# Gates and branch outputs of a hybrid decoder layer: the tokens' chunks as the stationary operand, 512 columns of weights moving

## The chip, the core and the metric

The kernel runs on one core of a Trainium2 chip. TensorE multiplies (a stationary operand of 128 by 128 is loaded, a moving operand streams past it, the result lands in PSUM); VectorE (DVE) and ScalarE (ACT) do elementwise work; SyncE (SP) issues the DMA transfers. The metric is the device time of one execution in microseconds (us).

## The reference, cut to what matters

One layer over 256 tokens with a model width of 2048, all in float32:

```python
mod = silu(c) @ w_ada + b_ada                       # six vectors of 2048
h = rmsnorm(x) * (1 + sc1) + sh1
proj = h @ w_in                                     # mixers' operands, then 3 * 2048 gate logits
y_pool, y_sb, y_gla = three mixers                  # widths 512, 1024, 512
gates = sigmoid(gate_logits)                        # (256, 3, 2048)
merged = gates[0] * (y_pool @ w_br_pool) + gates[1] * (y_sb @ w_br_sb) + gates[2] * (y_gla @ w_br_gla)
x = x + ga1 * (merged @ w_out)
h = rmsnorm(x) * (1 + sc2) + sh2
x = x + ga2 * ((silu(h @ w_ff_gate) * (h @ w_ff_up)) @ w_ff_down)
```

## The kernel before, in words

Activations are kept transposed: channels on the 128 partitions, 256 tokens along the free dimension. Each float32 operand is split into two float32r parts, hi and lo, and a product is the sum of three matmuls (hi·hi, hi·lo, lo·hi).

A piece of weights is at most 128 x 1056 (mostly 128 x 1024, 512 KB). `load` (L65) takes one of 6 raw buffers and issues the transfer on SP; `split_w` (L71) copies it to one of 3 hi buffers on ACT (L77) and subtracts into one of 3 lo buffers on DVE (L78). A raw buffer comes free when both are done, a hi or lo buffer when TensorE has used it up.

The stages, in the order of the program:
- the first norm with its modulation, and the mixers' operands (L205 to L277);
- `proj_v(w_vg, 528)` (L533), which already has the tokens' chunks as stationary operand, with 264 columns moving;
- the branch gates (`gates`, L558): 16 groups j of three blocks; a block of 128 gate columns is `block` (L94): 16 chunks of channels, three matmuls each with the weights stationary and 256 tokens moving, in one PSUM bank `acc` (4 banks). The first 8 groups (LEAD = 8) run ahead of the branch outputs, and the steps of the three mixers run between their blocks (`steps`);
- the loop over j (L592): the gates of group j + 8 (for j below 8), two pieces of w_br, 48 matmuls of 256 columns into three regions, three multiplications by the gates and two additions of 256 columns on DVE (L603 to L607), `split_x`, and the next of the modulation's columns;
- the output projection (L611 on, `block2`, whose matmuls are 512 and 256 columns wide in turn), the second norm, the feed-forward.

The modulation's remaining 128 pieces (`ada`, L181) are threaded through these stages. Each is a load of 512 KB into a raw buffer and one multiply-and-reduce on DVE (L173). `ADA = (1, 1, 4, 1, 1)` gives their numbers: one for each gate block, four after each branch output while j is below 8, one after that.

The order of instructions on each engine comes from a scheduler at compile time, which takes them by their place in the program as their inputs are ready by its own model; loads are issued on SP in program order as raw buffers come free. Each engine then runs its queue in that order.

Of the kernel before, what the change touches and what calls it, by code (L numbers as in the profile page):

```python
# [14 lines left out]
P = 128  # L15
# [11 lines left out]
# columns of the packed per-partition vectors  # L27
# [4 lines left out]
def kernel(ctx: ExitStack, tc: tile.TileContext, xT, c, vecs, consts, invc, masks, w_ada, w_per, w_ext,  # L32
# [38 lines left out]
    def split_w(src):  # L71
        """A weight piece as hi + lo, each exact in float32r."""
        n = src.shape[-1]
        raw = load(src)
        hi = whi.tile([P, WW], F32R, tag="hi", name=f"hi{next(names)}")[:, :n]
        lo = wlo.tile([P, WW], F32R, tag="lo", name=f"lo{next(names)}")[:, :n]
        nc.scalar.copy(hi, raw)  # L77
        vec.tensor_tensor(lo, raw, hi.bitcast(F32), ALU.subtract)  # L78
        return hi, lo

    def split_x(src, hi_scale=None):
        """[hi | lo] of a [128, 256] operand."""
        t = slot(F32R)
        nc.scalar.copy(t[:, :T], src)
        vec.tensor_tensor(t[:, T:], src, t[:, :T].bitcast(F32), ALU.subtract)
        return t
# [7 lines left out]
    def block(srcs, xs):  # L94
        """One 128-column block of a product: its transposed result in PSUM."""
        a = acc()
        n, i = len(xs), 0
        for src in srcs:
            hi, lo = split_w(src)
            for k in range(src.shape[-1] // P):  # L100
                mm3(a[:, :T], hi, lo, k, xs[i], i == 0, i == n - 1)
                i += 1
        assert i == n
        return a[:, :T]

    def mm2(out, hi, lo, k, x, first, last):
        """As mm3, in two terms that lie side by side and are still to be added."""
        mm(out, lhsT=hi[:, k * P:(k + 1) * P], rhs=x, start=first, stop=False, skip_group_check=True)  # L108
        mm(out[:, :T], lhsT=lo[:, k * P:(k + 1) * P], rhs=x[:, :T], start=False, stop=last, skip_group_check=True)  # L109
# [12 lines left out]
    def add_scaled(x, a, g):  # L122
        """x + g * a for a of two terms."""
        vec.scalar_tensor_tensor(x, a[:, T:], g, x, ALU.mult, ALU.add)
        vec.scalar_tensor_tensor(x, a[:, :T], g, x, ALU.mult, ALU.add)

    def rsqrt(m, t=None):
        """(m + eps) ** -0.5 of a mean of squares in PSUM, after one Newton step."""
        n = m.shape[-1]
        r, t = slot()[:, :n], (slot() if t is None else t)[:, :n]  # L130
        act(r, m, AF.Ln, bias=eps)
        act(r, r, AF.Exp, scale=-0.5)
        act(t, r, AF.Square)
        vec.scalar_tensor_tensor(t, m, EPS, t, ALU.add, ALU.mult)
        vec.tensor_scalar(t, t, -0.5, 1.5, ALU.mult, ALU.add)
        vec.tensor_tensor(r, r, t, ALU.mult)
        return r

# [66 lines left out]
    # ---- modulation of the first norm, chunk by chunk, and the columns of the mixers' operands: six pairs of  # L205
    # 128-column blocks stay in PSUM over all chunks, fourteen are summed in SBUF over groups of four chunks ----
# [161 lines left out]
    def odd(t, L):  # L368
        """The odd ones of the runs of L positions, for two heads of two blocks."""
        return t.rearrange("p (n two l) -> p n two l", two=2, l=L)[:, :, 1, :]  # L370

    def select(p, lv, k, q):
        """Scores of the pairs of positions that a level covers, for two heads of two blocks."""
        m = mx()
        w = q.shape[-1] // 4
        for i in range(4):
            mm(m[:, i * w:(i + 1) * w], lhsT=k[:, i * P:(i + 1) * P], rhs=q[:, i * w:(i + 1) * w], start=True,  # L377
               stop=True)
        mask, sc = mk[:, lv, :], scores[p]
        if w == P:  # L380
            sc, m = (t.rearrange("p (i t) -> p i t", i=4) for t in (sc, m))
            vec.copy_predicated(sc, mask.unsqueeze(1).broadcast_to([P, 4, P]), m)
        else:
            L = LEVELS[lv]
            n = w // L
            for i in range(4):
                vec.copy_predicated(odd(sc[:, i * P:(i + 1) * P], L), odd(mask, L),
                                    m[:, i * w:(i + 1) * w].rearrange("p (n l) -> p n l", l=L))
        left[p] -= 1
# [94 lines left out]
    # every mixer is a chain of steps; a step goes in two blocks or more after the one that feeds it  # L484
# [6 lines left out]
    LEAD, LIVE, LAG, ST, ST2 = 8, 5, 1, 3, 2  # L491
# [25 lines left out]
    def proj(n):  # L517
        return block([w_gate[n, 0], w_gate[n, 1]], h)

    def proj_v(src, n):  # L520
        """128 tokens by n columns, twice: the tokens' chunks as the stationary operand."""
        w = n if n <= 512 else n // 2
        m = [[acc() for _ in range(n // w)] for _ in range(2)]
        for i in range(8):
            hi, lo = split_w(src[i])
            for kk in range(2):
                k = 2 * i + kk
                for b in range(2):
                    xh, xl = h[k][:, b * P:(b + 1) * P], h[k][:, T + b * P:T + (b + 1) * P]
                    for xs, ws, f, l in ((xh, hi, k == 0, False), (xh, lo, False, False), (xl, hi, False, k == NK - 1)):  # L530
                        for c in range(n // w):
                            o = kk * n + c * w
                            mm(m[b][c][:, :w], lhsT=xs, rhs=ws[:, o:o + w], start=f, stop=l)  # L533
            if i % 2:
                steps(ST)
            ada(ADA[4])
# [6 lines left out]
    # v of the linear attention, with the 16 columns of its decay's rank behind it  # L543
    m = proj_v(w_vg, 528)
# [11 lines left out]
    merged, sigs = [], {}  # L556

    def gates(j):  # L558
        if j < NK:
            sigs[j] = []  # L560
            for i in range(3):
                r = proj(3 * j + i)
                if len(halves) < 1:
                    s = slot()
                    halves.extend((s[:, :T], s[:, T:]))
                s = halves.popleft()
                if unfinished():
                    nc.scalar.copy(s, r)
                    raw.append(s)
                else:  # L570
                    sigmoid[0] = act(s, r, AF.Sigmoid)
                ada(ADA[0] if j < LEAD else ADA[1])
                sigs[j].append(s)
                if unfinished():
                    steps(ST)

    halves, raw = deque(), []
    sigmoid = [None]
    for j in range(LEAD):
        gates(j)  # L580
# [11 lines left out]
    for j in range(NK):  # L592
        gates(j + LEAD)
        sig = sigs[j]
        hl = [split_w(w_br[j, i]) for i in range(2)]
        brs = [acc(), acc()]
        outs = [brs[0][:, :T], brs[0][:, T:], brs[1][:, :T]]
        for kk in range(NK):
            hi, lo = hl[kk // 8]
            b, lo_k, hi_k = (0, 0, 4) if kk < 4 else (1, 4, 12) if kk < 12 else (2, 12, 16)  # L600
            mm3(outs[b], hi, lo, kk % 8, ys[kk], kk == lo_k and b != 1, kk == hi_k - 1)
        m, t = slot(), slot()
        vec.tensor_tensor(m[:, :T], outs[0], sig[0], ALU.mult)  # L603
        vec.tensor_tensor(t[:, :T], outs[1], sig[1], ALU.mult)
        vec.tensor_tensor(m[:, :T], m[:, :T], t[:, :T], ALU.add)
        vec.tensor_tensor(t[:, :T], outs[2], sig[2], ALU.mult)
        vec.tensor_tensor(m[:, :T], m[:, :T], t[:, :T], ALU.add)  # L607
        merged.append(split_x(m[:, :T]))
        ada(ADA[2] if j + LEAD < NK else j < NK - 2)

# [1 line left out]
    with tc.issue_after(sigmoid[0].ins):  # L612
        nc.scalar.preload_act_table_set("natural_log_exp_and_others")
    # the first two blocks leave their last chunk, which is ready last, to the end
    firsts = [acc(), acc()]
    held = []
    for j in range(2):
        for half in range(2):
            hi, lo = split_w(w_out[j, half])
            for k in range(8 - half):  # L620
                mm2(firsts[j], hi, lo, k, merged[8 * half + k], k + half == 0, False)
        held.append((hi, lo))
    for j in range(2):
        mm2(firsts[j], *held[j], 7, merged[NK - 1], False, True)
# [43 lines left out]
    # the first three blocks go chunk by chunk, as the norm's chunks come  # L668
# [22 lines left out]
def _layouts(i):  # L691
# [5 lines left out]
    def blocks(w):  # L697
        """[K, N] -> [N/128][2][128][K/2 by 128]: per block of columns, the partition's rows in one run."""
# [3 lines left out]
    def cols(v):  # L702
# [18 lines left out]
    # pairs of 128 columns: q and k of each stick-breaking head, then q, k of the linear attention by two heads,  # L721
    # v of the stick-breaking heads, r of the linear attention and the channels of the pooling, two by two
# [14 lines left out]
        blocks(w_in[:, 5648:].reshape(D, 3, NK, P).transpose(0, 2, 1, 3).reshape(D, 3 * D)),  # L737
# [3 lines left out]
        blocks(w_br),  # L741
# [26 lines left out]
```

## Time and profile before

| | us |
|---|---|
| runs of the kernel: median of 3 (lowest, highest) | 1562.27 (1559.63, 1563.06) |
| profiled execution: span from first to last instruction | 1558.6 |
| median over this span | 3.7 |
| TensorE busy in the span | 1518.9 (97%) |
| VectorE busy | 1130.8 (73%) |
| ScalarE busy | 739.7 (47%) |

The trace gives the profiled execution by its span; no device time of its own is listed beside the three runs. The median of the runs lies 3.7 us above the span. Busy times count an instruction from start to end; matmuls are pipelined, so that a matmul's own duration is longer than the distance to the next one. The pace of a stretch is read from the starts.

### The profile page before, as it was taken

The page shows a single profiled execution, that of the slowest core. Times are in us where ns is not written, and L with a number is a line of the kernel's source. Part 1 is how long each engine was busy: PE and PEld are TensorE (multiplying, and loading weights), DVE is VectorE, ACT ScalarE, POOL GpSimd, SP SyncE. Part 2 cuts the span into 40 slices and gives each one's busy share as a digit, 9 for nine tenths or more (in the row PEclk, how much of TensorE's full clock was granted, in tenths as well). Part 3 has the DMA queues.
Part 4 walks back from the last instruction along what each step waited for, and adds up shares of the span by engine and source line. Part 5 has one row for each costly group of instructions (what it writes and reads, how often), then busy time and mean ns, then how long its engine had stood idle before and what let it go on. Part 6 is the DMA issues. An engine that isn't in the chain of part 4 may idle for free.

```text
span 1558.6 us, 26019 instructions
## 1 busy us (share of the span) xinstructions
PE 1518.9 (97%) x10304; PEld 1398.8 (90%) x10304; DVE 1130.8 (73%) x1671; ACT 739.7 (47%) x1028; POOL 1.9 (0%) x11
## 2 busy tenths in 40 slices
PE   5899999989999999999989999999999999999999
PEld 4899998989999999999877888888888888888888
DVE  7889979988877889898878666665555555545443
ACT  4454456465565434444445444444444444333333
POOL 0000000000000000000000000000000000000000
PEclk9899999999999999999999999999999999999999
DMA  9999984855768999997865777776666665666663
GB/s 329 372 328 326 332 276 136 287 193 194 243 215 280 323 342 345 351 314 230 285 208 196 234 239 229 241 230 188 189 189 189 188 189 176 207 192 202 190 207 95
DMA packets 108556, 377.17 MB, mean 242 GB/s; under 512 B 12049, under 2 KB 15249, under 8 KB 108433
## 3 DMA queue, kind: packets, MB, share of 16 engines
q1 hardware_dynamic: 108434, 375.52, 73.5%
q8 instruction: 80, 1.31, 0.3%
q14 instruction: 42, 0.34, 0.1%
HBM read 373.37 MB, written 2.10 MB: 241 GB/s over the span
## 4 chain that ended last, share of the span: by engine, by line
PE 91%; DVE 4%; DMA 2%; ACT 1%; issue 1%; SPq 0%; DVEq 0%; ACTq 0%
PE acc L108 34%; PE acc L109 18%; PE acc L92 9%; PE acc L90 9%; PE acc L91 9%; PE mx L90 3%; PE mx L91 3%; PE mx L92 3%; PE mx L239 3%; DVE raw L173 1%; PE acc L533 1%; DVE lo L78 1%; PE mx L377 1%; DMA raw<-in_w_ada_dram 1%; ACT s L39 1%
## 5 line engine op out<-in xcount | busy, mean ns | idle before, releaser
L78 DVE TENSOR_TENSOR lo<-raw,hi 128x1024 fp32r<-128x1024 f32 (+2 forms) x528 | 627.4, 1190 | 316.9 <-ACT hi L77 315.5
L77 ACT CAST hi<-raw 128x1024 fp32r<-128x1024 f32 (+2 forms) x528 | 539.3, 1023 | 653.6 <-issue 208.4
L108 PE MATMUL acc<-s,hi 128*128 128x512 f32 x2308 | 806.6, 394 | 5.5 <-DVE s L652 4.4
L109 PE MATMUL acc<-s,lo 128*128 128x256 f32 x2308 | 650.1, 282 | 1.2 <-DVE lo L78 1.1
L108 PEld LDWEIGHTS acc<-s,hi 128*128 128x128 f32 x2308 | 434.1, 188 | 104.5 <-issue 4.7
L109 PEld LDWEIGHTS acc<-s,lo 128*128 128x128 f32 x2308 | 434.7, 188 | 2.3 <-DVE lo L78 2.1
L90 PE MATMUL acc<-s,hi 128*128 128x256 f32 x1212 | 346.3, 286 | 14.2 <-ACT hi L77 14.1
L92 PE MATMUL acc<-s,lo 128*128 128x256 f32 x1212 | 344.6, 285 | 0.9 <-DVE lo L78 0.9
L91 PE MATMUL acc<-s,hi 128*128 128x256 f32 x1212 | 343.5, 284 | 0.0
L90 PEld LDWEIGHTS acc<-s,hi 128*128 128x128 f32 x1212 | 232.0, 191 | 16.3 <-ACT hi L77 15.6
L92 PEld LDWEIGHTS acc<-s,lo 128*128 128x128 f32 x1212 | 231.3, 191 | 2.9 <-DVE lo L78 2.2
L91 PEld LDWEIGHTS acc<-s,hi 128*128 128x128 f32 x1212 | 231.5, 191 | 0.2 <-issue 0.2
L173 DVE CUSTOM_DVE_ANT_0 raw<-raw,cs,mod 128x1024 f32<-128x1024 f32 x96 | 122.9, 1280 | 35.9 <-DMA raw<-in_w_ada_dram 35.1
L173 DVE CUSTOM_DVE_ANT_0 raw<-raw,cs,vt 128x1024 f32<-128x1024 f32 x96 | 122.8, 1279 | 29.3 <-DMA raw<-in_w_ada_dram 29.0
L90 PE MATMUL mx<-s,hi 128*128 128x256 f32 x384 | 110.0, 287 | 0.0
L91 PE MATMUL mx<-s,hi 128*128 128x256 f32 x384 | 108.3, 282 | 0.0
L92 PE MATMUL mx<-s,lo 128*128 128x256 f32 x384 | 108.0, 282 | 0.0
L39 ACT ACTIVATE s<-s 128x256 f32<-128x256 f32 (+2 forms) x167 | 83.5, 518 | 48.3 <-DVE s L662 34.7
L90 PEld LDWEIGHTS mx<-s,hi 128*128 128x128 f32 x384 | 73.2, 191 | 0.7 <-issue 0.5
L91 PEld LDWEIGHTS mx<-s,hi 128*128 128x128 f32 x384 | 72.8, 190 | 0.7 <-issue 0.7
L92 PEld LDWEIGHTS mx<-s,lo 128*128 128x128 f32 x384 | 72.7, 190 | 0.0
L239 PE MATMUL mx<-hi,s 128*128 128x256 f32 x256 | 47.4, 282 | 0.7 <-DVE s L302 0.7
(133 smaller groups left out, 780.5 us busy)
## 6 DMA issues: line engine op xcount, KB each, us to landing
raw<-in_w_ada_dram SPq DMA_DIRECT2D x192, 512.0 KB, 4.9
raw<-in_w_ff_dram SPq DMA_DIRECT2D x176, 512.0 KB, 4.2
raw<-in_w_gate_dram SPq DMA_DIRECT2D x96, 512.0 KB, 4.7
raw<-in_w_down_dram SPq DMA_DIRECT2D x80, 512.0 KB, 4.2
raw<-in_w_ext_dram SPq DMA_DIRECT2D x56, 512.0 KB, 5.2
raw<-in_w_br_dram SPq DMA_DIRECT2D x32, 512.0 KB, 5.0
raw<-in_w_out_dram SPq DMA_DIRECT2D x32, 512.0 KB, 4.5
raw<-in_w_per_dram SPq DMA_DIRECT2D x32, 384.0 KB, 5.0
```

The source lines that it names most:

```text
L39: r = nc.scalar.activation(out, in_, func, **kw)
L77: nc.scalar.copy(hi, raw)
L78: vec.tensor_tensor(lo, raw, hi.bitcast(F32), ALU.subtract)
L90: mm(out, lhsT=wh, rhs=x[:, :T], start=first, stop=False, skip_group_check=True)
L91: mm(out, lhsT=wh, rhs=x[:, T:], start=False, stop=False, skip_group_check=True)
L92: mm(out, lhsT=wl, rhs=x[:, :T], start=False, stop=last, skip_group_check=True)
L108: mm(out, lhsT=hi[:, k * P:(k + 1) * P], rhs=x, start=first, stop=False, skip_group_check=True)
L109: mm(out[:, :T], lhsT=lo[:, k * P:(k + 1) * P], rhs=x[:, :T], start=False, stop=last, skip_group_check=True)
L173: vec.tensor_tensor_reduce(raw, raw, cs[:, i * 1024:(i + 1) * 1024], 1.0, init, ALU.mult, ALU.add, mod[:, t, i:i + 1])
L239: mm(m[:, b * T:(b + 1) * T], lhsT=l, rhs=r, start=first and i == 0, stop=last and i == 2, skip_group_check=True)
L377: mm(m[:, i * w:(i + 1) * w], lhsT=k[:, i * P:(i + 1) * P], rhs=q[:, i * w:(i + 1) * w], start=True, stop=True)
L533: mm(m[b][c][:, :w], lhsT=xs, rhs=ws[:, o:o + w], start=f, stop=l)
```

## The change

Gate logits and branch outputs are computed with the activations' chunks (128 channels by 128 tokens) as the stationary operand and 512 columns of hi or lo weights as the moving one, by a `proj_v` that takes any operand list. The results have tokens on partitions, in two banks of 512 columns. There are now 4 groups g of 512 columns in place of 16 groups of 128; two groups of gates run ahead. The mixers' steps are taken after every second piece inside `proj_v`, the modulation's pieces after every second piece of gates (`every=2`), and in the branch loop in one run after each of the three branches: 4, 8 and 4 for the first two groups, 1, 2 and 1 for the last two. The merged result is turned back, in 128 x 128 blocks, by `nc.tensor.transpose` into a PSUM bank `mx` and split from there; the turn of a group stands behind the first branch of the next one. The first two blocks of the output projection leave their last four chunks to the end, in place of the last one. The weights on the host are laid out to match, in pieces of the same size (128 x 1024).

```diff
-    def proj(n):
-        return block([w_gate[n, 0], w_gate[n, 1]], h)
-
-    def proj_v(src, n):
-        """128 tokens by n columns, twice: the tokens' chunks as the stationary operand."""
+    def proj_v(src, n, x=h, every=1):
         w = n if n <= 512 else n // 2
         m = [[acc() for _ in range(n // w)] for _ in range(2)]
-        for i in range(8):
+        last = 2 * len(src) - 1
+        for i in range(len(src)):
             hi, lo = split_w(src[i])
             for kk in range(2):
                 k = 2 * i + kk
                 for b in range(2):
-                    xh, xl = h[k][:, b * P:(b + 1) * P], h[k][:, T + b * P:T + (b + 1) * P]
-                    for xs, ws, f, l in ((xh, hi, k == 0, False), (xh, lo, False, False), (xl, hi, False, k == NK - 1)):
+                    xh, xl = x[k][:, b * P:(b + 1) * P], x[k][:, T + b * P:T + (b + 1) * P]
+                    for xs, ws, f, l in ((xh, hi, k == 0, False), (xh, lo, False, False), (xl, hi, False, k == last)):
                         for c in range(n // w):
                             o = kk * n + c * w
                             mm(m[b][c][:, :w], lhsT=xs, rhs=ws[:, o:o + w], start=f, stop=l)
-            if i % 2:
+            if i % 2 and unfinished():
                 steps(ST)
-            ada(ADA[4])
+            ada(i % every == every - 1)
         return m
...
-    def gates(j):
-        if j < NK:
-            sigs[j] = []
+    NG, LEAD_G = 4, 2
...
+    def gates(g):
+        if g < NG:
+            sigs[g] = []
             for i in range(3):
-                r = proj(3 * j + i)
-                if len(halves) < 1:
-                    s = slot()
-                    halves.extend((s[:, :T], s[:, T:]))
-                s = halves.popleft()
-                if unfinished():
-                    nc.scalar.copy(s, r)
-                    raw.append(s)
-                else:
-                    sigmoid[0] = act(s, r, AF.Sigmoid)
-                ada(ADA[0] if j < LEAD else ADA[1])
-                sigs[j].append(s)
-                if unfinished():
-                    steps(ST)
+                m = proj_v([w_gate[i, g, n] for n in range(8)], 512, every=2)
+                s = [slot(), slot()]
+                for b in range(2):
+                    if unfinished():
+                        nc.scalar.copy(s[b], m[b][0])
+                        raw.append(s[b])
+                    else:
+                        sigmoid[0] = act(s[b], m[b][0], AF.Sigmoid)
+                sigs[g].append(s)
...
-    for j in range(NK):
-        gates(j + LEAD)
-        sig = sigs[j]
-        hl = [split_w(w_br[j, i]) for i in range(2)]
-        brs = [acc(), acc()]
-        outs = [brs[0][:, :T], brs[0][:, T:], brs[1][:, :T]]
-        for kk in range(NK):
-            hi, lo = hl[kk // 8]
-            b, lo_k, hi_k = (0, 0, 4) if kk < 4 else (1, 4, 12) if kk < 12 else (2, 12, 16)
-            mm3(outs[b], hi, lo, kk % 8, ys[kk], kk == lo_k and b != 1, kk == hi_k - 1)
-        m, t = slot(), slot()
-        vec.tensor_tensor(m[:, :T], outs[0], sig[0], ALU.mult)
...
-        merged.append(split_x(m[:, :T]))
-        ada(ADA[2] if j + LEAD < NK else j < NK - 2)
+    def turn(ms, c):
+        m = mx()
+        for i in range(4):
+            nc.tensor.transpose(m[:, i * P:(i + 1) * P], ms[i % 2][:, (c + i // 2) * P:(c + i // 2 + 1) * P], ident)
+        for i in range(2):
+            merged.append(split_x(m[:, i * T:(i + 1) * T]))
+
+    waiting = []
+    for g in range(NG):
+        gates(g + LEAD_G)
+        ms = [slot(), slot()]
+        for i, (k0, k1) in enumerate(((0, 4), (4, 12), (12, 16))):
+            o = proj_v([w_br[g, n] for n in range(k0 // 2, k1 // 2)], 512, ys[k0:k1], 8)
+            ada((4 if g + LEAD_G < NG else 1) * (k1 - k0) // 4)
+            for b in range(2):
+                s = sigs[g][i][b]
+                vec.tensor_tensor(s if i else ms[b], o[b][0], s, ALU.mult)
+                if i:
+                    vec.tensor_tensor(ms[b], ms[b], s, ALU.add)
+            if i == 0:
+                while waiting:
+                    turn(*waiting.pop(0))
+        waiting += [(ms, 0), (ms, 2)]
...
-            for k in range(8 - half):
+            for k in range(8 - 4 * half):
                 mm2(firsts[j], hi, lo, k, merged[8 * half + k], k + half == 0, False)
         held.append((hi, lo))
+    while waiting:
+        turn(*waiting.pop(0))
     for j in range(2):
-        mm2(firsts[j], *held[j], 7, merged[NK - 1], False, True)
+        for k in range(4, 8):
+            mm2(firsts[j], *held[j], k, merged[8 + k], False, k == 7)
```

## Rows read from the trace of the kernel before

**Rows 1.** The page, part 1: busy time, share of span, instructions.

```profile
PE 1518.9 (97%) x10304; PEld 1398.8 (90%) x10304; DVE 1130.8 (73%) x1671; ACT 739.7 (47%) x1028; POOL 1.9 (0%) x11
```

**Rows 2.** Busy time by stretch: PE, PEld, DVE, ACT, POOL; clock; DMA share, GB/s.

```profile
450.00:490.00 40.00, 40.00 (x333) 39.52 (x333) 32.03 (x45) 28.07 (x52) 0.00 (x0) 1.00 0.76 244
530.00:570.00 40.00, 39.39 (x331) 39.19 (x331) 34.52 (x54) 17.24 (x22) 0.00 (x0) 1.00 0.95 334
610.00:650.00 40.00, 40.00 (x339) 40.00 (x339) 35.26 (x50) 16.91 (x21) 0.00 (x0) 1.00 0.96 354
650.00:700.00 50.00, 50.00 (x424) 50.00 (x423) 46.32 (x74) 23.04 (x28) 0.00 (x0) 1.00 0.93 323
```

**Rows 3.** Chain of work that ended last: start us, us, what.

```profile
246.36 0.60 DVE s L247
...
348.40 1.78 PE mx L353 x16
...
525.63 1.19 DVE raw L173
526.84 1.14 DVE lo L78
528.00 6.99 DMA raw<-in_w_ada_dram
535.16 1.07 issue
536.64 1.14 DVE lo L78
537.83 0.38 PE acc L92
```

**Rows 4.** Timeline of PE, 690 to 712.9: first two and last.

```profile
689.74 0.28 PE L90 MATMUL acc<-s,hi 128*128 128x256 f32 x1
689.86 0.28 PE L91 MATMUL acc<-s,hi 128*128 128x256 f32 x1
...
712.89 0.28 PE L90 MATMUL acc<-s,hi 128*128 128x256 f32 x1
```

**Rows 5.** Timeline of PE, 1000 to 1034: first two and last.

```profile
999.76 0.40 PE L108 MATMUL acc<-s,hi 128*128 128x512 f32 x1
999.99 0.28 PE L109 MATMUL acc<-s,lo 128*128 128x256 f32 x1
...
1033.92 0.39 PE L108 MATMUL acc<-s,hi 128*128 128x512 f32 x1
```

**Rows 6.** Groups by line and shape: busy us, mean ns; idle before, releasers.

```profile
L77 ACT CAST hi<-raw 128x1024 fp32r<-128x1024 f32 x472 | 494.2, 1048 | 585.4 <-issue 208.4 <-PE acc L108 159.6 <-PE acc L91 124.9
L78 DVE TENSOR_TENSOR lo<-raw,hi 128x1024 fp32r<-128x1024 f32 x472 | 575.8, 1222 | 294.9 <-ACT hi L77 293.5
L247 DVE TENSOR_TENSOR s<-s,mx 128x512 f32<-128x512 f32 x42 | 28.6, 682 | 8.8 <-PE mx L92 7.2 <-PE mx L239 1.3
L606 DVE TENSOR_TENSOR s<-acc,s 128x256 f32<-128x256 f32 x16 | 6.7, 417 | 0.2
L353 PE MATMUL mx<-ct,s 128*128 128x128 f32 x16 | 1.9, 275 | 0.0
```

**Rows 7.** Timeline of DVE, 540 to 548.

```profile
540.83 2.35 DVE L78 TENSOR_TENSOR lo<-raw,hi 128x1024 fp32r<-128x1024 f32 x2
545.00 1.28 DVE L173 CUSTOM_DVE_ANT_0 raw<-raw,cs,mod 128x1024 f32<-128x1024 f32 x1 [1.82 <-DMA raw<-in_w_ada_dram]
546.21 0.08 DVE L173 DVE_READ_ACCUMULATOR2_ANT mod<- 128x1 f32 x1
546.21 1.28 DVE L173 CUSTOM_DVE_ANT_0 raw<-raw,cs,vt 128x1024 f32<-128x1024 f32 x1
547.42 0.08 DVE L173 DVE_READ_ACCUMULATOR2_ANT mod<- 128x1 f32 x1
```

**Rows 8.** Timeline of SP's queue, 536 to 553.

```profile
536.34 1.79 SPq L68 DMA_DIRECT2D raw<-in_w_br_dram  x2
539.39 4.14 SPq L68 DMA_DIRECT2D raw<-in_w_ada_dram  x4
546.32 1.53 SPq L68 DMA_DIRECT2D raw<-in_w_gate_dram  x2
548.66 0.33 SPq L68 DMA_DIRECT2D raw<-in_w_ada_dram  x1
549.99 1.47 SPq L68 DMA_DIRECT2D raw<-in_w_gate_dram  x2
```

**Rows 9.** Transfers of the gates' weights, from issue to landing.

```profile
DMA to landing us min/median/max: 3.3/4.7/7.1
```

**Rows 10.** Waits of PE, longest in total first.

```profile
PE acc L90 <- ACT hi L77: 14.1, 5, 7.2
PE acc L108 <- DVE s L652: 4.4, 1, 4.4
PE mx L643 <- ACT s L39: 3.0, 1, 3.0
```

More of the change, by code (lines that the diff above doesn't have):

```diff
@@ L490 @@
     clock = [0]
-    LEAD, LIVE, LAG, ST, ST2 = 8, 5, 1, 3, 2
+    LIVE, LAG, ST, ST2 = 5, 1, 3, 2
     ADA = (1, 1, 4, 1, 1)
@@ L542 @@
         steps(ST2, 2.6)
-    m = proj_v(w_vg, 528)
+    m = proj_v([w_vg[i] for i in range(8)], 528)
     at = slot()
@@ L554 @@
     steps(ST)
-    merged, sigs = [], {}
-    def gates(j):
-        if j < NK:
-            sigs[j] = []
-            for i in range(3):
-                r = proj(3 * j + i)
-                if len(halves) < 1:
-                    s = slot()
-                    halves.extend((s[:, :T], s[:, T:]))
-                s = halves.popleft()
-                if unfinished():
-                    nc.scalar.copy(s, r)
-                    raw.append(s)
-                else:
-                    sigmoid[0] = act(s, r, AF.Sigmoid)
-                ada(ADA[0] if j < LEAD else ADA[1])
-                sigs[j].append(s)
-                if unfinished():
-                    steps(ST)
[L577 to L580, printed above, removed]
+    NG, LEAD_G = 4, 2
+    merged, sigs, raw = [], {}, []
+    sigmoid = [None]
+    def gates(g):
+        if g < NG:
+            sigs[g] = []
+            for i in range(3):
+                m = proj_v([w_gate[i, g, n] for n in range(8)], 512, every=2)
[7 more added lines that the diff above has]
+                sigs[g].append(s)
+    for g in range(LEAD_G):
+        gates(g)
     while unfinished():
@@ L591 @@
     ys = [*y_pool, *y_sb, *y_gla]
-    for j in range(NK):
-        gates(j + LEAD)
-        sig = sigs[j]
-        hl = [split_w(w_br[j, i]) for i in range(2)]
-        brs = [acc(), acc()]
-        outs = [brs[0][:, :T], brs[0][:, T:], brs[1][:, :T]]
-        for kk in range(NK):
-            hi, lo = hl[kk // 8]
-            b, lo_k, hi_k = (0, 0, 4) if kk < 4 else (1, 4, 12) if kk < 12 else (2, 12, 16)
-            mm3(outs[b], hi, lo, kk % 8, ys[kk], kk == lo_k and b != 1, kk == hi_k - 1)
-        m, t = slot(), slot()
-        vec.tensor_tensor(m[:, :T], outs[0], sig[0], ALU.mult)
[L604 to L607, printed above, removed]
-        merged.append(split_x(m[:, :T]))
-        ada(ADA[2] if j + LEAD < NK else j < NK - 2)
+    def turn(ms, c):
[20 more added lines that the diff above has]
+        waiting += [(ms, 0), (ms, 2)]
     with tc.issue_after(sigmoid[0].ins):
@@ L736, in _layouts @@
         con(pair[6:].reshape(14, 4, 4, P, 256).transpose(0, 1, 3, 2, 4)).reshape(14, 4, P, 1024),
-        blocks(w_in[:, 5648:].reshape(D, 3, NK, P).transpose(0, 2, 1, 3).reshape(D, 3 * D)),
+        con(w_in[:, 5648:].reshape(8, 2, P, 3, 4, 512).transpose(3, 4, 0, 2, 1, 5)).reshape(3, 4, 8, P, 1024),
         con(vg.reshape(8, 2, P, 528).transpose(0, 2, 1, 3)).reshape(8, P, 1056),
@@ L740, in _layouts @@
         con(i["w_pool"][0]),
-        blocks(w_br),
+        con(w_br.reshape(8, 2, P, 4, 512).transpose(3, 0, 2, 1, 4)).reshape(4, 8, P, 1024),
         blocks(i["w_out"][0]),
```

## The prediction

> **What bounds the kernel now.** I read the page's busy shares first: TensorE is busy 97% of the span, VectorE 73% [rows 1]. Then the table by stretches over the gates and branch outputs, which run from about 317 to 713 us: in the four stretches shown TensorE idles 0.6 us of 40 in one and not at all in the others [rows 2], and the waits of TensorE there are few in number [rows 10]. So the stage is bound by how fast matmuls follow each other. What the reader is to see as well is how near two other things are to their limits. From 610 to 650 us the DMA engines are 96% busy at 354 GB/s; from 650 to 700 us VectorE is busy 46.3 of 50 us [rows 2]. And the one stall, at 537 us, goes back in the chain of waits to a late modulation piece and the split queued behind it [rows 3]. The cover over DMA and VectorE is thin.
>
> **The matmuls.** The gates have 48 blocks of 48 matmuls, the branch outputs 16 of 48: 3072 matmuls of 256 columns. After the change the same columns go in 12 x 96 + 4 x 96 = 1536 matmuls of 512. The pace of 256 columns: 195 steps from 689.74 to 712.89 us, so 0.1187 us each [rows 4]. The pace of 512 columns has a row where 512 and 256 alternate: 98 pairs from 999.76 to 1033.92 us, 0.3486 us a pair [rows 5]; less 0.1187 that is 0.2299. Two of 256 cost 0.2374, one of 512 costs 0.2299, and 1536 x 0.0076 = 11.7 us are saved: 353.0 instead of 364.7 us. The granted clock is 1.00, the 2.4 GHz level [rows 2], so 512 columns can't go under 0.2133: the saving lies between 0 (512 costs twice 256) and 37 us. I take 11.7, since its row has this very shape.
>
> The Trainium skill (TensorE: Matmul & The Clock Gate, Back-to-back issue gap) gives 262 cycles for 256 columns and 518 for 512: only some 2.5 ns saved per pair, an estimate of 3.8 us over 1536, which speaks against the change. The trace doesn't agree with it on the size: 118.7 and 229.9 ns against its 109 and 216, so matmuls here carry more than that fixed cost.
>
> **The turns.** 8 turns of 4 transposes, 32 in all, which before has none of. The nearest row is a plain matmul of 128 columns in f32: 16 in 1.78 us on the chain, 0.111 each [rows 3], against 0.275 for the duration of one by itself [rows 6]. So 3.6 us, up to 8.8 if none overlaps. I take 3.6: four stand together, and three groups' turns stand in the middle of matmuls that don't need them. The last group's stand behind 24 pairs of the first two output blocks, 8.4 us, which cover its last two multiplications and two additions (2.4 us) and the split.
>
> **Evacuation.** Before, a group of 128 columns takes five VectorE instructions of 256 columns [rows 6] and a split; after, a group of 512 takes ten of 512. The row for 512 columns from PSUM is 0.682 us long [rows 6] and 0.60 to the next [rows 3]: 6.0 us per group. In total VectorE is not loaded more (4 x 6.0 against 16 x 5 x 0.34). The gates are read from PSUM by ACT in both, in half as many instructions of twice the width. PSUM is neither freer nor tighter: two calls of two banks stand in place of four blocks of one.
>
> **What doesn't change in sum.** 128 pieces of weights stay 128 pieces of 512 KB; the modulation takes 94 pieces up to the output projection before, 96 after; the mixers' steps come after every second piece, as before after every block. Costed at nothing, as the same engines do the same number in the same stage.
>
> **What moves.** The modulation's pieces gather. Before, each j below 8 loads 8 weights and 7 modulation pieces in 192 x 0.1187 = 22.8 us of matmuls, never more than 4 modulation pieces together [rows 8]. A piece is 0.524 MB, at 354 GB/s 1.48 us, so 15 take 22.2 us: it just fits. After, the gates of one group take 36 pieces in 66.2 us, 53.3 of DMA; then the branches of one group take 8 weights and 16 modulation pieces in 96 x 0.2299 = 22.1 us of matmuls: 35.5 us of DMA, and on VectorE 8 splits of 1.13 (two in 2.35 [rows 7], of which the second takes 1.22 [rows 6]), 16 reductions of 1.21 [rows 7] and 6.0 of evacuation, 34.4 us. The slack of the gates before it can be used only as far as buffers reach.
>
> I count that for the first branches, from TensorE's start on them. By then two weights are split ahead, four more lie in raw buffers, the first run of 4 is through, and two of the run of 8 hold the last raw buffers. Still to come before the next call's first weight are 6 modulation pieces, 2 weights and 4 more modulation pieces: with it, 13. The first can be issued when a buffer is reduced, at 1.2; 13 x 1.48 = 19.2; and the shortest landing, 3.3 us [rows 9], has 1.8 beyond the transfer. It lands at 22.2 at the earliest and is cast (1.05 [rows 6]) and split (1.13) at 24.4. TensorE wants it at 22.1 + 0.2. So at least 2.1 us of stall. Following the six buffers one by one with the median landing of 4.7, the third branch's first weight is late by about 1 and the next call's by about 4. I take 5 us for the first branches and 5 for the second, whose successor is the third group's branches. After that the runs are 1, 2, 1 and VectorE needs about 21 of 23 us. Lower bound 4.2 for both, or 0 if the scheduler has reordered more than I see; upper bound 16 (below).
>
> **The sum.** -11.7 + 3.6 + 10 = +1.9 us. On the profiled span of 1558.6 that gives 1560.5; the runs' median lies 3.7 above the span, so 1564.2, which I round to 1564. A measurement of this kernel can tell about 0.2%, 3.1 us, from no change, so this is "no change that shows".
>
> **The rivals.**
> First, faster: the burst is mostly hidden. For it: in the stretch of 96% DMA TensorE lost nothing [rows 2], because two splits and the raw buffers lie between. Against it: 24 pieces in 22 us are far more than 15 in 22.8. With the floor of 4.2 us: -11.7 + 3.6 + 4.2 = -3.9, 1558; with nothing lost, 1554. It decides below 2.5 us of stall per group.
> Second, slower: VectorE's queue. When the second branch ends, its two multiplications and additions (2.4 us) come ahead of the split of the third branch's first weight in the program, and the same happens at the end of the third branch ahead of the next call's split. If VectorE is late, each goes in front of a split that TensorE waits for: about 3.6 and 4.2 us per group, 15.6 for two. -11.7 + 3.6 + 15.6 = +7.5, 1570. For it: the stall at 537 us is of this kind [rows 3]. It decides once VectorE is more than a split behind when the second branch ends.
> Third, the pace of 512 after 512 is better than in alternation. With the 12 ns that 256 columns carry over the clock's 106.7, 512 would take 0.2253: a saving of 18.6, net -5, 1557. Nothing in the trace has 512 after 512 in float32r.
> Fourth, halving the count saves a small fixed cost only, and what 256 columns carry goes with the columns: a saving of some 3.8 us, net +9.8, 1572. That is what the rule above would do here; against it stand the two paces.
>
> **How the numbers follow.** Forecast (stalls of 7 to 13 us) 0.34, hidden burst 0.30, VectorE's queue 0.22, better pace 0.09, small fixed cost 0.05. Faster by over 0.2%: two thirds of the hidden burst and the better pace, near 0.30. Slower: the last third of the forecast, the queue and the fixed cost, 0.39. The rest, 0.31, is within 0.2%. The range reaches from the hidden burst with nothing lost (1554, less 1 for a better pace) to the queue with further 6 us for a third group: 1553 to 1576. The forecast's own range is 1561 to 1567.
>
> **What would show it.** Starts of 512-column matmuls 0.230 us apart; transposes 0.11 apart, in fours; TensorE idle in two places, at the end of the first and second groups' branches, released by a split or cast that waits for its transfer behind a run of modulation pieces; no other new idle time of over 1 us. It would be wrong if the pace is off by 5 ns either way (8 us), if the stalls don't come, or if the mixers' steps, now inside `proj_v`, hold TensorE where they didn't.

## The result, and the profile after

The changed kernel takes 1580.4 us (median of 4 runs, 1577.4 to 1583.6), the kernel before 1561.3 (1559.6 to 1563.1) beside it: a ratio of 1.0131, interval 1.0117 to 1.0145. It is slower by 1.3%, some 20 us, and lies above the range that was given (1553 to 1576).

The page of the changed kernel, part 1, for [rows 1]:

```profile
PE 1521.5 (96%) x8800; PEld 1328.3 (84%) x8800; DVE 1128.1 (71%) x1631; ACT 735.8 (47%) x993; POOL 1.9 (0%) x11
```

TensorE has 1504 instructions fewer and is busy no less. The stage by itself, from the first gate matmul to the first of the output projection, in the table by stretches (first the kernel before, second the changed one; span of the stretch, then the busy times of PE, PEld, DVE, ACT and POOL, clock, DMA share, GB/s):

```profile
317.30:715.03 397.73, 395.40 (x3288) 391.31 (x3289) 338.57 (x551) 198.63 (x287) 0.98 (x2) 1.00 0.82 281
```

```profile
315.02:733.05 418.03, 397.22 (x1778) 321.12 (x1777) 337.00 (x513) 194.35 (x249) 0.53 (x1) 0.98 0.80 269
```

The stage is 20.3 us longer. TensorE idles 20.8 us in it (the span less PE's busy time), where it idled 2.3; and its granted clock is 0.98, where it was 1.00. VectorE, ScalarE and the DMA engines have no more to do in sum than before. The waits of TensorE that are new, from the list of waits (us in total, times, longest):

```profile
PE acc L531 <- DVE lo L78: 9.0, 6, 2.8
PE acc L531 <- ACT hi L77: 7.9, 3, 3.5
...
PE mx L590 <- DVE s L605: 2.5, 4, 1.3
```

L531 is the matmul in `proj_v`, L590 the transpose, L605 the addition that closes a branch. The longest of the six waits for a split comes ahead of the first run of modulation pieces, in the third group's gates. VectorE stood at a reduction that waited 2.67 us for its load, and the split was queued behind it (timelines of PE and DVE):

```profile
488.75 0.80 PE L531 MATMUL acc<-lo,s 128*128 128x512 f32 x1 [2.81 <-DVE lo L78]
484.99 1.29 DVE L173 CUSTOM_DVE_ANT_0 raw<-raw,cs,vt 128x1024 f32<-128x1024 f32 x1 [2.67 <-DMA raw<-in_w_ada_dram]
```

The kernel before has no such wait there. The worst places are the first two groups' third branch and what follows. Here is TensorE at the first of them (timeline):

```profile
569.30 0.40 PE L531 MATMUL acc<-hi,s 128*128 128x512 f32 x1
572.50 0.73 PE L531 MATMUL acc<-hi,s 128*128 128x512 f32 x2 [2.81 <-ACT hi L77]
575.04 0.80 PE L531 MATMUL acc<-lo,s 128*128 128x512 f32 x1 [1.81 <-DVE lo L78]
575.64 0.63 PE L531 MATMUL acc<-hi,s 128*128 128x512 f32 x1
```

A weight is cast late (2.8 us), then split late (1.8 us). SP's queue of the same time, for [rows 8], shows what stands ahead of it:

```profile
549.08 3.93 SPq L68 DMA_DIRECT2D raw<-in_w_br_dram  x4
553.88 10.80 SPq L68 DMA_DIRECT2D raw<-in_w_ada_dram  x8
565.68 1.53 SPq L68 DMA_DIRECT2D raw<-in_w_br_dram  x2
568.10 4.79 SPq L68 DMA_DIRECT2D raw<-in_w_ada_dram  x4
575.02 2.07 SPq L68 DMA_DIRECT2D raw<-in_w_gate_dram  x2
```

The eight modulation pieces after the second branch take 10.8 us to issue, and only then, at 565.68, come the third branch's two weights, which TensorE wants right behind the matmul of 569.30. The next gates' first pair is issued at 575.02, after the last run of four. VectorE meanwhile (timeline, for [rows 7]):

```profile
564.37 1.28 DVE L173 CUSTOM_DVE_ANT_0 raw<-raw,cs,vt 128x1024 f32<-128x1024 f32 x1
565.57 0.08 DVE L173 DVE_READ_ACCUMULATOR2_ANT mod<- 128x1 f32 x1
565.57 1.28 DVE L173 CUSTOM_DVE_ANT_0 raw<-raw,cs,vt 128x1024 f32<-128x1024 f32 x1
...
571.25 1.28 DVE L173 CUSTOM_DVE_ANT_0 raw<-raw,cs,mod 128x1024 f32<-128x1024 f32 x1
...
573.17 0.68 DVE L603 TENSOR_TENSOR s<-acc,s 128x512 f32<-128x512 f32 x1
573.77 1.22 DVE L78 TENSOR_TENSOR lo<-raw,hi 128x1024 fp32r<-128x1024 f32 x1
```

From 564.4 to 573.8 it does reductions and evacuations without a gap; the split that TensorE waits for is the last of them. So DMA and VectorE are both full at the place where TensorE is starved.

What the stall leaves behind is in the table by stretches of 5 us:

```profile
560.00:570.00 10.00, 9.69 (x43) 7.56 (x41) 10.00 (x18) 1.05 (x1) 0.00 (x0) 1.00 0.97 348
570.00:575.00 5.00, 0.73 (x2) 0.30 (x2) 5.00 (x10) 2.10 (x2) 0.00 (x0) 0.87 1.02 411
575.00:580.00 5.00, 4.96 (x12) 3.90 (x13) 5.00 (x7) 0.50 (x1) 0.00 (x0) 0.50 0.96 339
590.00:595.00 5.00, 5.00 (x23) 4.05 (x23) 4.32 (x6) 1.87 (x2) 0.00 (x0) 1.00 0.94 356
```

From 575 to 580 TensorE is busy again, but at a granted clock of 0.50, the 1.2 GHz level, and does 12 matmuls where 23 fit at the full clock (590 to 595).

The pace itself is as hoped. Three matmuls of a chunk, from 504.84 to 519.40 us (the timeline merges equal neighbours; it is 63 steps from the first to the last):

```profile
504.84 0.39 PE L531 MATMUL acc<-lo,s 128*128 128x512 f32 x1
505.06 0.63 PE L531 MATMUL acc<-hi,s 128*128 128x512 f32 x2
...
519.40 0.39 PE L531 MATMUL acc<-lo,s 128*128 128x512 f32 x1
```

That is 14.56 / 63 = 0.2311 us, against 0.2299 assumed and 0.2374 for two of 256 [rows 4].

### The profile page after: what moved, and what is told of

Its sections match the earlier page's. It is cut to its first block, busy times and chain, and to the rows that moved or that the text cites. A ratio compares the mean times of both kernels' runs of the same rounds, so it can differ in the third digit from the quotient of the medians.

```text
span 1580.0 us, 22931 instructions
## 1 busy us (share of the span) xinstructions
PE 1521.5 (96%) x8800; PEld 1328.3 (84%) x8800; DVE 1128.1 (71%) x1631; ACT 735.8 (47%) x993; POOL 1.9 (0%) x11
## 4 chain that ended last, share of the span: by engine, by line
PE 76%; DVE 10%; DMA 8%; issue 4%; ACT 1%; DVEq 0%; SPq 0%; ACTq 0%
PE acc L108 33%; PE acc L109 17%; PE acc L531 12%; DMA raw<-in_w_ada_dram 7%; DVE raw L173 3%; DVE lo L78 3%; PE mx L239 3%; PE mx L92 2%; PE mx L90 2%; PE mx L91 2%; PE acc L92 1%; PE acc L90 1%; PE acc L91 1%; PE mx L377 1%; DMA raw<-in_w_ext_dram 1%
## 5 line engine op out<-in xcount | busy, mean ns | idle before, releaser
L77 ACT CAST hi<-raw 128x1024 fp32r<-128x1024 f32 (+2 forms) x528 | 540.2, 1024 | 677.6 <-issue 208.6
L109 PE MATMUL acc<-s,lo 128*128 128x256 f32 x2308 | 650.0, 282 | 1.9 <-DVE lo L78 1.9
L108 PEld LDWEIGHTS acc<-s,hi 128*128 128x128 f32 x2308 | 434.8, 188 | 105.2 <-issue 4.8
L109 PEld LDWEIGHTS acc<-s,lo 128*128 128x128 f32 x2308 | 435.6, 189 | 3.4 <-DVE lo L78 2.8
L531 PE MATMUL acc<-hi,s 128*128 128x512 f32 (+1 forms) x1152 | 352.0, 388 | 7.9 <-ACT hi L77 7.9
L531 PEld LDWEIGHTS acc<-hi,s 128*128 128x128 f32 x1152 | 213.6, 191 | 54.2 <-ACT hi L77 9.0
L531 PE MATMUL acc<-lo,s 128*128 128x512 f32 (+1 forms) x576 | 217.9, 387 | 9.0 <-DVE lo L78 9.0
L531 PEld LDWEIGHTS acc<-lo,s 128*128 128x128 f32 x576 | 107.9, 191 | 33.2 <-DVE lo L78 11.7
L39 ACT ACTIVATE s<-s 128x512 f32<-128x512 f32 (+2 forms) x156 | 81.9, 537 | 55.9 <-DVE s L665 37.5
L90 PE MATMUL acc<-s,hi 128*128 128x256 f32 x188 | 54.7, 293 | 14.2 <-ACT hi L77 14.2
L92 PE MATMUL acc<-s,lo 128*128 128x256 f32 x188 | 54.4, 296 | 0.7 <-DVE lo L78 0.5
L91 PE MATMUL acc<-s,hi 128*128 128x256 f32 x188 | 54.2, 290 | 0.0
```

What stands on the lines that cost most here:

```text
L39: r = nc.scalar.activation(out, in_, func, **kw)
L90: mm(out, lhsT=wh, rhs=x[:, :T], start=first, stop=False, skip_group_check=True)
L91: mm(out, lhsT=wh, rhs=x[:, T:], start=False, stop=False, skip_group_check=True)
L92: mm(out, lhsT=wl, rhs=x[:, :T], start=False, stop=last, skip_group_check=True)
```

## The experiments

Two theories stood at first. A: the modulation's pieces, gathered into runs of 4, 8 and 4, starve the branches' weights. B: reading out two banks of 512 columns and turning the result hold TensorE by themselves. Four kernels decide between them.

**The same pieces spread within the same groups (e1_spread).**

```diff
-                m = proj_v([w_gate[i, g, n] for n in range(8)], 512, every=2)
+                m = proj_v([w_gate[i, g, n] for n in range(8)], 512, every=2 if g < LEAD_G else 1)
...
-            ada((4 if g + LEAD_G < NG else 1) * (k1 - k0) // 4)
+            ada((k1 - k0) // 4)
```

> The changed kernel with the same number of modulation pieces in each group, but one after every piece of the third and fourth groups' gates (24 in place of 12) and 1, 2, 1 after the branches in place of 4, 8, 4. Theory A, the runs of modulation pieces starve the branch weights of raw buffers and DMA and fill VectorE: the waits of TensorE in the first two groups' branches (some 20 us, and the half clock that follows them, some 7 us) mostly go, 1556 to 1563 us; a little stays, as a group's 60 pieces take 88.8 us of DMA in 88.3 us of matmuls. Theory B, reading out two banks of 512 columns and turning the result holds TensorE whatever the modulation does: 1575 to 1582 us.

Measured: 1552.2 us, 0.9958 of the kernel before (0.9943 to 0.9973). It is faster than both kernels. The table by stretches for its stage:

```profile
315.95:704.94 388.99, 387.65 (x1777) 316.47 (x1777) 336.88 (x513) 193.75 (x249) 0.53 (x1) 1.00 0.83 289
```

TensorE idles 1.3 us, the clock is 1.00, with the same matmuls, transposes and evacuations. Against this row the changed kernel's 29.0 us more are 19.5 of idle time and 9.6 of busy time; the work on TensorE is the same but for one record. Of the 9.6, some 7.2 are matmuls at the lower clock, an estimate from how much further apart than 0.231 us they start. The rest fits the matmuls just ahead of a wait, which count their whole 0.39 us. Not all of the 29.0 us stands behind the runs. The wait of 2.8 us at 488 us stands ahead of them, as do 2.8 of the 7.2 us at the lower clock: 1.5 behind that wait and 1.3 at the start of the stage. That DMA is 0.99 busy in one stretch (490 to 530 us) costs TensorE nothing:

```profile
490.00:530.00 40.00, 40.00 (x175) 32.45 (x174) 36.18 (x51) 17.20 (x19) 0.00 (x0) 1.00 0.99 376
```

B is out.

**The pieces moved forward to the first two groups' gates (e2_early).**

```diff
-                m = proj_v([w_gate[i, g, n] for n in range(8)], 512, every=2)
+                m = proj_v([w_gate[i, g, n] for n in range(8)], 512, every=1 if g < LEAD_G else 2)
...
-            ada((4 if g + LEAD_G < NG else 1) * (k1 - k0) // 4)
+            ada((k1 - k0) // 4)
```

> The changed kernel with 24 modulation pieces more in the first two groups' gates (one after every piece), where the DMA engines are 65 to 73% busy, and 1, 2, 1 after every branch; 96 in all up to the output projection, as before. Theory A: no run is left and no stretch asks for more DMA than there is, 1551 to 1557 us, clear below the kernel before. Theory B: 1575 to 1582 us.

Measured: 1565.4 us, 1.0041 (1.0026 to 1.0056). Both were missed, A by 8 us. The waits at the branches are gone, as A said (0.3 us is left). But TensorE waits 2.4 us for a split in the third group's gates (at 493 us), and in the first two groups, where the mixers' steps run, it now idles more:

```profile
293.00:330.00 37.00, 32.00 (x178) 26.88 (x177) 34.62 (x72) 18.29 (x30) 0.53 (x1) 0.91 0.63 208
...
410.00:450.00 40.00, 38.38 (x191) 31.25 (x190) 38.88 (x83) 22.12 (x31) 0.00 (x0) 1.00 0.84 283
```

I had read that stage's slack from its DMA share alone. VectorE was busy 35 to 36 of 37 to 40 us in parts of it already; from 410 to 450 it is busy 38.9 of 40 here. In the spread version TensorE idles 2.0 us in the first of these stretches, at a clock of 1.00, and nothing in the second. The 1.6 us of the second are waits for a split and a cast of the gates' own weights (1.0 and 0.6), the waits of the first are at the mixers' matmuls. That a full VectorE is the cause of both is argued from these rows, not tested by itself.

**Half the runs (e3_half).**

```diff
-            ada((4 if g + LEAD_G < NG else 1) * (k1 - k0) // 4)
+            ada((2 if g + LEAD_G < NG else 1) * (k1 - k0) // 4)
```

> The changed kernel with 2, 4, 2 modulation pieces after the first two groups' branches in place of 4, 8, 4; 16 pieces go to later stages. Theory A: a group's branches then take 16 pieces, 23.7 us of DMA in 22.1 us of matmuls, and the waits there fall from some 20 us to under 6: 1558 to 1566 us. Theory B: 1575 to 1582 us.

Measured: 1561.0 us, 1.0004 (0.9994 to 1.0013), as A said: no change from the kernel before.

**The same gathering in the kernel before (e4_bunch_before).**

```diff
-        ada(ADA[2] if j + LEAD < NK else j < NK - 2)
+        ada((16 if j % 4 == 3 else 0) if j + LEAD < NK else j < NK - 2)
```

> The kernel before with its modulation pieces after the branch outputs gathered: 16 after every fourth column group in place of 4 after each, while gates are still computed. Theory A: each of the two runs takes 23.7 us of DMA and 19.4 us of VectorE ahead of the next gate block's weights, against some 10 us that are split or lie in raw buffers: 8 to 15 us lost per run, 1575 to 1592 us. Theory B: no change, 1558 to 1565 us.

Measured: 1602.0 us, 1.0275 (1.0260 to 1.0291), 10 us above A's range. The table by stretches at the two runs:

```profile
570.00:610.00 40.00, 27.07 (x204) 26.57 (x204) 35.01 (x60) 10.21 (x13) 0.00 (x0) 0.83 0.96 347
...
700.00:740.00 40.00, 31.58 (x238) 31.28 (x239) 35.58 (x60) 14.12 (x16) 0.00 (x0) 0.81 0.88 313
```

With not one matmul changed, gathering alone costs 42 us, and the clock falls here too. So it belongs to the modulation's place and not to the 512 columns.

Next, the price of the parts, and what it is in a run that starves the weights. On the spread version:

**Each transpose made twice (e5_turn_twice).**

```diff
         for i in range(4):
             nc.tensor.transpose(m[:, i * P:(i + 1) * P], ms[i % 2][:, (c + i // 2) * P:(c + i // 2 + 1) * P], ident)
+        for i in range(4):
+            nc.tensor.transpose(m[:, i * P:(i + 1) * P], ms[i % 2][:, (c + i // 2) * P:(c + i // 2 + 1) * P], ident)
```

> The spread version (e1_spread) with each of the 32 transposes made twice, the second over the first, so that only TensorE's part is doubled. If a transpose costs its place in the row of eight (0.87 us for 8 in the trace of e1_spread): 3.5 us more, 1555 to 1557 us. If each costs the duration of one by itself, 0.275: 8.8 us more, 1560 to 1562 us.

Measured: 1555.1 us, 0.9975 (0.9964 to 0.9987): 0.0017 above the spread version's ratio, some 2.7 us, with intervals that allow 0 to 6. It fits the 3.5 us and not the 8.8; it can't be told from no change. Eight in a row in the spread version (timeline of PE):

```profile
571.69 1.03 PE L590 MATMUL mx<-ct,s 128*128 128x128 f32 x8
```

One lasts 0.27 us, so seven steps take 0.76: 0.109 each, 0.87 for eight.

**Matmuls of 512 made as two of 256 (e8_halves).**

```diff
+                            if w == 512:
+                                for q in range(0, 512, T):
+                                    mm(m[b][c][:, q:q + T], lhsT=xs, rhs=ws[:, o + q:o + q + T], start=f and q == 0,
+                                       stop=l, skip_group_check=True)
+                                continue
                             mm(m[b][c][:, :w], lhsT=xs, rhs=ws[:, o:o + w], start=f, stop=l)
```

> The spread version (e1_spread) with each matmul of 512 columns in gates and branches made as two of 256 with the same stationary operand, loaded twice: 3072 matmuls as in the kernel before. If the pace of 512 is what the change brings, two of 256 cost 0.0063 to 0.0076 us more each time: 9.7 to 11.7 us more, 1561 to 1565 us, the kernel before plus its turns. If matmuls of either width cost the same per column, no change: 1551 to 1555 us.

Measured: 1564.5 us, 1.0036 (1.0022 to 1.0050): 12.3 us above the spread version and clear of no change. Its stage, from the first gate matmul on:

```profile
315.41:716.80 401.39, 396.20 (x3313) 392.01 (x3314) 336.23 (x513) 194.41 (x249) 0.53 (x1) 1.00 0.81 281
```

That is 12.4 us longer than the spread version's: 8.6 of busy time, which is the pace, and 3.9 of idle time, most of it three waits for a split (3.1 us in all). So the 12.3 us hold more than the pace; by busy time the wider matmul is worth 8.6, by the distances of the starts 9.7 us. No other gain of the change was found.

On the changed kernel, the runs taken apart. The helper is the same in three kernels, called for the runs of the first two groups only; the sums of these 32 pieces are left out in part (e6, e9) or wholly (e7).

```diff
+    def thin(t, i):
+        raw = load(w_ada[t, i])
+        init = vt[:, V_ADA + t:V_ADA + t + 1] if i == 0 else mod[:, t, 0:1]
+        vec.tensor_tensor_reduce(raw[:, :64], raw[:, :64], cs[:, i * 1024:i * 1024 + 64], 1.0, init, ALU.mult, ALU.add,
+                                 mod[:, t, i:i + 1])
```

**Full loads, reductions of 64 columns (e6_run_loads)**, as above.

> The changed kernel with its runs of 4, 8, 4 modulation pieces loaded in full, but reduced over 64 of 1024 columns only (most of these pieces' sums is left out): the runs keep their DMA and raw buffers and lose nearly all of their VectorE time. Theory A1, the runs hurt by DMA and raw buffers: the waits stay, 1572 to 1582 us. Theory A2, they hurt by VectorE's queue, splits and evacuations behind reductions: most waits go, 1553 to 1562 us.

**Loads of 64 columns, full reductions (e7_run_reductions).**

```diff
+        raw = wraw.tile([P, WW], F32, tag="raw", name=f"raw{next(names)}")[:, :1024]
+        nc.sync.dma_start(raw[:, :64], w_ada[t, i][:, :64])
...
+        c = cs[:, i * 1024:(i + 1) * 1024]
+        vec.tensor_tensor_reduce(raw, c, c, 1.0, init, ALU.mult, ALU.add, mod[:, t, i:i + 1])
```

> The changed kernel with its runs of 4, 8, 4 modulation pieces loading 64 of 1024 columns and reducing 1024 columns of another tile in their place (these pieces' sums are left out): the runs keep VectorE's time and the number of raw buffers taken, and lose nearly all of their DMA. A1, DMA: most waits go, 1553 to 1562 us. A2, VectorE's queue: the waits stay, 1572 to 1582 us. If both run out at once, each of the two brings part: 1562 to 1572 us in both.

**Loads of 64 columns, reductions of 64 (e9_run_thin).**

```diff
+        raw = load(w_ada[t, i][:, :64])
```

> The changed kernel with its runs of 4, 8, 4 modulation pieces loading 64 of 1024 columns and reducing these 64 (most of these pieces' sums is left out): the runs keep their places in SP's and VectorE's queues and their raw buffers, and lose both DMA and VectorE time. If the runs hurt by DMA and VectorE running out together: most waits of TensorE in the branches go, 1552 to 1558 us. If they hurt by holding raw buffers from issue to reduction, whatever they carry: the waits stay, 1564 to 1576 us.

Measured: full loads alone 1570.5 us (1.0090, 1.0065 to 1.0115); full reductions alone 1576.2 (1.0116, 1.0099 to 1.0132); neither 1555.4 (0.9977, 0.9966 to 0.9988), near the spread version. The full loads came out below the range that A1 gave and inside that of both running out at once, the full reductions inside A2's. So either resource by itself starves the weights. Against the 0.0154 between the changed kernel and the one with neither, full loads alone keep 0.0113 of the loss and full reductions alone 0.0139; the last can't be told from the whole. The runs' places in the queues and in the raw buffers, with nothing in them to carry, cost some 3 us by the difference to the spread version (0.0019), with intervals that allow 0 to 6. The wait ahead of the runs, at 487 us, is still there in this kernel, with 0.95 us, so it doesn't come from what the runs carry. The issue of the eight pieces suggests why one doesn't do for the other (SP's queue; e6, then e7):

```profile
547.88 10.92 SPq L68 DMA_DIRECT2D raw<-in_w_ada_dram  x8
```

```profile
549.30 11.69 SPq L183 DMA_DIRECT2D raw<-in_w_ada_dram  x8
```

They take 10.9 and 11.7 us, as the 10.8 of the changed kernel: a raw buffer seems to come round at the pace of a transfer in the one, and of a reduction between splits in the other, which are near the same. That is argued from these rows.

**The transposes held back to their place in the program (e10_turn_late).** In TensorE's queue of the changed kernel the first two groups' transposes stand right behind their own group's matmuls, 2.5 us of waits.

```diff
-                    turn(*waiting.pop(0))
+                    with tc.issue_after(latest[0]):
+                        turn(*waiting.pop(0))
```

(`latest[0]` is the last matmul of the branch.)

> The changed kernel with the transposes of a group held behind the last matmul of the next group's first branch in TensorE's queue, where the program has them; in the changed kernel the scheduler drew the first two groups' ahead, next to their own last additions. If TensorE's waits ahead of those transposes (0.9 and 1.3 us, and 0.4 and 1.6 us behind) are a loss of their own: 2 to 5 us less than the changed kernel, 1575 to 1579 us. If the time is only waited for elsewhere, ahead of the next group's first weights: 1579 to 1583 us.

Measured: 1581.8 us, 1.0145 (1.0129 to 1.0160), no gain. Where the transposes stood, the split of the next weights is now waited for by 2.7 us (timeline of PE):

```profile
583.29 0.50 PE L533 MATMUL acc<-lo,s 128*128 128x512 f32 x1 [2.65 <-DVE lo L78]
```

The wait at the transposes was no loss of its own. The scheduler had put them into a gap that was there anyway.

## Why the prediction was wrong

**The pace** was right in kind and somewhat too large: 11.7 us were forecast, and 512 columns go at 0.2311 where 0.2299 was taken, which makes it 9.7. e8 has 8.6 by busy time. So 512 after 512 is no faster than in alternation; the third rival had 0.2253. The prediction had weighed an estimate from the Trainium skill (TensorE: Matmul & The Clock Gate, Back-to-back issue gap), 3.8 us; the measurement decides against it for this kernel.

**The turns** were right: 3.6 us forecast, 8 transposes take 0.87 us, 3.5 for 32, and e5 agrees.

**Evacuation, and what doesn't change in sum**, were right: e1 leaves them and TensorE idles 1.3 us in the stage.

**What moves** was right in its mechanism and its main places: the runs of modulation pieces, at the first two groups' branches, the split or cast behind them. Its size was wrong, and that is the step that failed. "I take 5 us for the first branches and 5 for the second": TensorE idles 7.5 us at the first and 9.1 at the second, 16.6 in all, and loses some 4.4 more there at the lower clock, by the estimate above. The 10 us were taken halfway between a floor of 4.2 and a ceiling of 16, and even the ceiling was passed. The floor of 2.1 us a group was reckoned from DMA alone; VectorE had been counted too (34.4 us in 22.1), but then went into a rival. The rows were 1.6 times the matmuls' time on both; e6 and e7 show that each by itself is enough for more than half the loss. The rival of VectorE's queue, at 15.6 us of waits, was the nearer one; it had 0.22. "No other new idle time of over 1 us" failed as well: 2.8 us were waited at 488 us, ahead of the runs. The spread version doesn't have this wait; why the changed kernel has it stays open.

**What was missing** is the clock. No term of the sum and no rival had it: some 7.2 us of matmuls at the lower level in the stage, 4.4 behind the runs' waits, 1.5 behind the wait at 488 us, 1.3 at the start. With what was measured the sum for the stage is -9.7 for the pace, +2.6 for the 24 transposes that stand in it, +29.0 between the spread and the changed kernel, -1.0 for waits that only the kernel before had (2.3 against 1.3 us): +20.9, where +20.3 was measured. In the profiled executions the changed kernel is 2.3 us shorter ahead of the stage (315.02 against 317.30) and 3.4 longer behind it, 21.4 in all; these two weren't traced further.

So the change with its pieces spread is worth 0.42%, some 7 us (e1 against before, interval 4 to 9). The pieces' place in the changed kernel costs some 27 us (1.0131 against 0.9958), of which what the runs carry is some 24 (1.0131 against 0.9977, e9).

## What to carry to other kernels

Wider matmuls are a gain only as large as the starts of both widths in the trace say, here 2 to 3% of the stage, and no more than a few starved stretches can cost. When a loop is made coarser, whatever was threaded through it (loads for a later stage, reductions on another engine) must be threaded through the new inner loop, not be run once per coarse step: here the sum over the stage fitted and didn't show the loss; the sum over one group's branches, 35 us of DMA and 34 of VectorE in 22 of matmuls, did. Before moving such work to an idle-looking stage, read every engine's busy time there, not only the one that was full.

## What the runs showed of the hardware

The price of a wait of TensorE was more than the wait. In the changed kernel the two waits of 2.8 and 1.8 us, with two matmuls between them, were followed by a stretch of 5 us at a granted clock of 0.50, and matmuls of 512 columns 0.42 to 0.43 us apart (from 575.64 over 576.07 to 576.49) in place of 0.231:

```profile
576.07 0.63 PE L531 MATMUL acc<-lo,s 128*128 128x512 f32 x1
576.49 1.05 PE L531 MATMUL acc<-hi,s 128*128 128x512 f32 x2
```

Over the stage, some 7 us of lower clock came with 19.5 us of waits, more than a third as much again. A single wait was enough for it: behind the 2.81 us at 488 us the clock was 0.82 from 490 to 495 us. Single waits of 1.25 and 1.5 us (649 and 548 us) left the clock at 1.00 in the rows around them. The length of the wait alone doesn't decide: at the same place, 1.79 us in e3 brought the clock down (0.83 from 490 to 495 us) and 2.10 us in e7 didn't (1.00). What does decide, these runs don't show. Transposes in float32, eight in a row, go 0.109 us apart, though each lasts 0.27 from start to end (571.69 us in the spread version).
